# A modulated norm folded into the evacuation of the first projection, at the two places where a whole row must be known first

## The chip, the core and the metric

The kernel runs on one core of a Trainium2 chip. The metric is the device time of one execution in microseconds (us). TensorE (PE in the profile) multiplies matrices into PSUM; VectorE (DVE), ScalarE (ACT) and GpSimd (POOL) do the rest; SyncE (SP) issues the DMAs. Each engine works through its own instructions in their order.

## The reference, cut to what matters

Two blocks of two layers each run on 256 tokens of width 2048, in float32. The first block ends in `rmsnorm(x, norm_f)`. The second block then does, with `c` a conditioning vector:

```
shift, scale, gate = split(silu(c) @ ada_w[i] + ada_b[i], 3)
h = rms_norm(x, norm_g[i]) * (1 + scale) + shift
layer 0:  u, v, z = split(h @ a_w_in, 3);  out = (gelu(u) * mix(layer_norm(gelu(v))) * silu(z)) @ a_w_out
layer 1:  h_kv = rms_norm(x, kv_norm_g) * (1 + kv_scale) + kv_shift
          c_kv, k_r = split(h_kv @ kv_w_dkv);  c_q, z = split(h @ b_w_in);  attention ... @ b_w_out
x = x + gate * out
```

So `h @ W` needs, for each token, the root mean square of a whole row of `x`, and the last quarter of that row comes out of the projection just before it.

## The kernel before

Every float32 product is made of three matmuls: each factor is split into a high part (float32r) and a low part, and `mm3` (L307, L308, L309) adds high by high, low weight by high, and high weight by low. Weights come in chunks of two 128-row tiles by 512 columns (512 KB). A chunk is one step of a `Stream`: twelve matmuls, two tiles by two token halves (t = 0, 1) by three products. A projection onto 512 columns is eight steps, and its result is two PSUM banks (one per half). Each step begins with `begin()`, which writes for the engines, in this order: the high part of a later chunk (L254, ACT, tile wh), due tasks (`after(d, ...)` puts a task d steps ahead), one waiting transpose set (`trq`), the low part of that chunk (L264, DVE, tile wl), due conditioning multiplications (L428, the products silu(c) @ ada_w done on DVE row by row from 512 KB pieces, araw), and DMA fetches. wh and wl are made `ahead` chunks early (4 normally) and have five buffers each; raw weights (wraw) have five as well, which some of the conditioning pieces share. `clk["rate"]` is the number of conditioning pieces fetched per step; when all are read, the generator `ada_gen` is at its end.

Two places need the norm of a whole row while the next projection is due. Both are written as a `crossing` of two streams with half t = 1 lagging two steps. The first goes from `ob3` (the last projection of block 1) to `gv0` and `gv1`, whose chunks alternate in pairs; the second from `go13` to `cq` and `z0`. In it, `evac` adds the residual and squares, `stats` sums the squares and takes the power on POOL, `row_bcast` (L806) spreads the factor over partitions with a matmul (tile inv_row), `evac_tr` transposes the last block (L376, tiles x3tr and x4tr), and `mod_split` multiplies by the factor (L817, tile hx), adds the shift and splits into high (L821, hgH or h2H) and low (L824, hgL or h2L). Between the two crossings `ahead` is 4, inside them it is 2. In the second one the same is done for the key/value input (kv2H, kv2L), then follow `dkv`, the narrow `dkr` (48 matmuls), the query projections `uq` and the key/value projections `ukv`, which need `lora_norm` of cq and of dkv (transposes cqtr, ckvtr).

Of the kernel before, what the change touches and what calls it, by code (L numbers as in the profile page):

```python
# [46 lines left out]
def tile_kernel(ctx: ExitStack, tc: tile.TileContext, A: dict, out: bass.AP):  # L47
# [99 lines left out]
    plan_pair(a_w_in, GW, a_w_in, GW + NB, 8)  # L147
    for j in range(2, 8):
        plan(a_w_in, GW + j * NB)
# [249 lines left out]
    for i in range(2):  # L399
        gd = dram.tile([1, D], F32, name=f"gate{i}")  # L400
        gates.append(gd)

    def store_row(src, dst, name):

        def cp(pt):
            row = T2(nm(name))
            dve.tensor_copy(row[:16, :P], pt[:16, 0, :])
            after(1, lambda: sp.dma_start(dst[0].rearrange("(k p) -> k p", p=P), row[:16, :P]))
        through(3, name, lambda pt: pe.transpose(pt[:16, 0, :], src, ident), cp)
# [3 lines left out]
    def ada_vec(key, W, n0):  # L413
# [5 lines left out]
        def part(j, half):  # L419
# [7 lines left out]
            def mul():  # L427
# [3 lines left out]
                if (j, half) == (15, 1):  # L431
                    if key[:2] == "ga":
                        store_row(d, gates[int(key[2])], "gate_row")
                    done.add(key)
# [5 lines left out]

    def ada_all():
        for key, W, n0 in (("sh0", adaw[0], 0), ("sc0", adaw[0], D), ("ga0", adaw[0], 2 * D),
                           ("kvsh", A["kv_ada_w"], 0), ("kvsc", A["kv_ada_w"], D),
                           ("sh1", adaw[1], 0), ("sc1", adaw[1], D), ("ga1", adaw[1], 2 * D)):
            yield from ada_vec(key, W, n0)

# [357 lines left out]
    def row_bcast(r, pb):  # L804

        pe.matmul(pb, r[:, 0:1].to_broadcast([P, P]), ident, start=True, stop=True)  # L806
        return pb

    def mod_split(z, rbs, sh, H, L, ts, k0, k1):

        w = len(ts) * P
        t0 = ts[0] * P
        n = 4 // len(ts)
        for ka in range(k0, k1, n):
            tmp = T2(nm("hx")).rearrange("p (a b) -> p a b", a=n)
            for i, t in enumerate(ts):
                dve.tensor_mul(tmp[:, :, i * P:(i + 1) * P], z[:, ka:ka + n, t * P:(t + 1) * P],  # L817
                               rbs[t].unsqueeze(1).to_broadcast([P, n, P]))
            for i in range(n):
                k = ka + i  # L820
                act.activation(H[:, k, t0:t0 + w], tmp[:, i, :], AF.Identity, bias=sh[:, k:k + 1])  # L821
            for i in range(n):
                k = ka + i
                dve.scalar_tensor_tensor(L[:, k, t0:t0 + w], tmp[:, i, :], sh[:, k:k + 1],  # L824
                                         H[:, k, t0:t0 + w].bitcast(F32), op0=OP.add, op1=OP.subtract)

    def crossing(s0, s1, z, sh, evac, evac_tr, stats, fin, then=lambda i, rbs: None):

        n0, n1 = len(s0.order), len(s1.order)
        rbs = []
        pb = sc_p.tile([P, 1024], F32, tag="sc", name=nm("inv_row"))
        pieces = {1: ((0,), 4, 8), 2: ((1,), 0, 4), 3: ((1,), 4, 8),
                  5: ((0, 1), 8, 10), 6: ((0, 1), 10, 12), 7: ((0, 1), 12, 14), 8: ((0, 1), 14, 16)}
        clk["ahead"] = LAG
        for i in range(len(s0)):
            if i == n0:  # L840
                evac(s0.ps[0][0], 0)
            if i == n0 + 1:
                rbs.append(stats(0, pb[:, 0:P]))
                evac_tr(0)
            s0.step(i)
        evac(s0.ps[0][1], 1)
        mod_split(z, rbs, sh, s1.H, s1.L, (0,), 0, 4)
        rbs.append(stats(1, pb[:, NB:NB + P]))
        evac_tr(1)
        for i in range(n1 // 2 + 1):  # L850
            if i in pieces:
                mod_split(z, rbs, sh, s1.H, s1.L, *pieces[i])
            s1.step(i)
        last = max(i for i, o in enumerate(s1.order) if o[0] == 0)
        for i in range(n1 // 2 + 1, len(s1)):
            then(i - n1 // 2 - 1, rbs)
            s1.step(i)
            if i == last + s1.lag:
                fin(0, s1.ps[0])
        fin(1, s1.ps[1])  # L860
        clk["ahead"] = AHEAD

    x3d = dram.tile([S, D], F32, name="x3d")
    z3 = B16(F32, "z3")
    ssq2, ssq3 = [ST(f"ssq_x2{t}") for t in range(T)], [ST(f"ssq_x3{t}") for t in range(T)]
# [3 lines left out]
    class Ob:  # L869
# [23 lines left out]
        def evac_tr(self, t):  # L893
            cols_mul(z3, transpose_block(self.xf[t], "x3tr"), gm0[0], self.j, t)

        def whole(self, ps):
            def go():
                for t in range(T):
                    self.evac(ps[t], t)
                for t in range(T):  # L900
                    tr_then(2 + t, self.xf[t], "x3tr", lambda pt, t=t: cols_mul(z3, pt, gm0[0], self.j, t))
            after(1, go)

    def stats_f(t, pb):

        s = ST(nm("s23"))
        dve.tensor_reduce(s[:, 0:1], ssq2[t][:, :4], axis=AX.X, op=OP.add)
        dve.tensor_scalar(s[:, 2:3], s[:, 0:1], EPS / D, EPS * EPS, op0=OP.mult, op1=OP.add)
        dve.tensor_reduce(s[:, 1:2], ssq3[t][:, :4], axis=AX.X, op=OP.add)
        dve.scalar_tensor_tensor(s[:, 2:3], s[:, 1:2], 1.0 / D, s[:, 2:3], op0=OP.mult, op1=OP.add)  # L910
        pool.tensor_tensor(s[:, 3:4], s[:, 2:3], mhalf[:, 0:1], op=OP.pow)
        inv1.append(rstd(s[:, 0:1], 1, D, "inv_f"))
        return row_bcast(s[:, 3:4], pb)
# [14 lines left out]
    clk["rate"] = 0.0  # L928
    ob = Ob(3, 6)
    hH, hL = B16(F32R, "hgH"), B16(F32R, "hgL")  # L930
    vg = [big.tile([P, GW], F32, tag="b16", name=f"vg{t}") for t in range(T)]
    bst = [const.tile([P, 8, 6], F32, name=f"bst{t}") for t in range(T)]

    def gv_evac(j, ps):
        js = slice(j * NB, (j + 1) * NB)

        def gelu():
            for t in range(T):
# [5 lines left out]
        after_each(1, gelu, bn)  # L944
# [18 lines left out]
    for j in range(2, 8):  # L963
# [55 lines left out]
    def lora_norm(ps, gname, name, fast=False):  # L1019
# [6 lines left out]
        def copy():  # L1026
            for t in range(T):
# [34 lines left out]
    class Go:  # L1062
# [23 lines left out]
        def evac_tr(self, t):  # L1086
            pt = transpose_block(self.xb[t], "x4tr")
            cols_mul(z1, pt, gms[1], self.j, t)
            cols_mul(zk, pt, gms[0], self.j, t)

        def whole(self, ps):
            def cols(t, pt):
                cols_mul(zk, pt, gms[0], self.j, t)
                cols_mul(z1, pt, gms[1], self.j, t)

            for t in range(T):
                after(1, lambda t=t: self.evac(ps[t], t))
# [46 lines left out]
    zk, z1 = B16(F32, "zk"), B16(F32, "z1")  # L1144

# [460 lines left out]
```

## Time and profile before

| quantity | value |
|---|---|
| median of 3 runs | 2146.68 us (2146.36 to 2148.63) |
| the profiled execution | 2146.95 us, its span 2145.2 us |
| mean granted TensorE clock | 0.994 of full speed |
| PE, weight loads, DVE, ACT, POOL busy | 98%, 81%, 73%, 47%, 1% of the span |
| instructions | 26773 |
| DMA | 538.27 MB, mean 251 GB/s |

The span runs from the first to the last instruction; the execution has 1.75 us around it. Busy shares are means over stages, and matmuls overlap in the record (each lasts 0.39 us and starts 0.23 us after the one before), so a busy PE says little by itself: what counts is where the start of one matmul is late.

### The profile page before, as it was taken

The numbers are of one execution on the slowest core, as the hardware profiler recorded it, in microseconds if no ns is written. First come the engines' busy times: TensorE is split into PE (matmuls) and PEld (weight loads), VectorE is DVE, ScalarE is ACT, GpSimd is POOL, SyncE is SP. The second block draws the span as 40 slices with busy tenths as digits, with TensorE's granted clock in tenths as the row PEclk, the third lists the DMA queues.
The fourth block names the chain that finished last, engine by engine and source line by source line (L and its number), as shares of the span: only waits on it lengthen the run. The fifth ranks groups of instructions, "written<-read, shape, count | busy, mean of one in ns | idle before, by whom it ended". The sixth has DMA issues, their size and how long they took to land.

```text
span 2145.2 us, 26773 instructions
## 1 busy us (share of the span) xinstructions
PE 2097.5 (98%) x9646; PEld 1729.2 (81%) x9646; DVE 1564.8 (73%) x2277; ACT 1011.6 (47%) x1364; POOL 31.0 (1%) x25
## 2 busy tenths in 40 slices
PE   8999999999999999998999999999999988999999
PEld 6888888888888888886788888888888866788787
DVE  6677788877776776675688888878888767666555
ACT  6444454444545444554544444434344445666442
POOL 0000000000000000000000000000000000110000
PEclk9999999999999999999999999999999999999999
DMA  8788987898755554575699889899889845444455
GB/s 323 277 290 298 307 293 275 300 337 286 245 195 197 187 196 153 188 264 202 219 354 339 316 293 322 316 315 338 286 312 324 279 152 163 150 136 130 128 175 177
DMA packets 157733, 538.27 MB, mean 251 GB/s; under 512 B 17792, under 2 KB 18848, under 8 KB 157088
## 3 DMA queue, kind: packets, MB, share of 16 engines
q1 hardware_dynamic: 157600, 536.56, 72.7%
q8 instruction: 76, 1.25, 0.2%
q14 instruction: 57, 0.47, 0.1%
HBM read 525.99 MB, written 10.50 MB: 250 GB/s over the span
## 4 chain that ended last, share of the span: by engine, by line
PE 52%; DVE 3%; ACT 2%; issue 1%; POOL 0%; ACTq 0%; POOLq 0%; DVEq 0%
PE gz L309 3%; PE gz L307 3%; PE gu L307 3%; PE gu L309 3%; PE gz L308 3%; PE gu L308 3%; PE go L309 3%; PE go L307 3%; PE go L308 3%; PE gv L308 2%; PE gv L309 2%; PE gv L307 2%; PE o L309 1%; PE o L308 1%; PE o L307 1%; PE ob L307 1%
## 5 line engine op out<-in xcount | busy, mean ns | idle before, releaser
L254 ACT ACTIVATE wh<-wraw 128x1024 fp32r<-128x1024 f32 (+2 forms) x698 | 734.4, 1054 | 1031.3 <-issue 145.7
L264 DVE TENSOR_TENSOR wl<-wraw,wh 128x1024 fp32r<-128x1024 f32 (+2 forms) x698 | 846.8, 1218 | 399.6 <-ACT wh L254 395.2
L428 DVE CUSTOM_DVE_ANT_0 araw<-araw,silu_c,vec 128x1024 f32<-128x1024 f32 x128 | 163.8, 1280 | 3.3 <-DMA araw<-in_ada_w 3.1
L307 PE MATMUL q<-wh,hbH 128*128 128x512 f32 x384 | 155.3, 405 | 0.0
L309 PE MATMUL q<-wh,hbL 128*128 128x512 f32 x384 | 150.4, 392 | 0.0
L308 PE MATMUL q<-wl,hbH 128*128 128x512 f32 x384 | 149.7, 390 | 0.0
L308 PE MATMUL gv<-wl,hgH 128*128 128x512 f32 x256 | 100.7, 393 | 1.8 <-DVE wl L264 1.8
L307 PE MATMUL gu<-wh,hgH 128*128 128x512 f32 x256 | 102.0, 398 | 0.0
L307 PE MATMUL gz<-wh,hgH 128*128 128x512 f32 x256 | 101.6, 397 | 0.0
L307 PE MATMUL gv<-wh,hgH 128*128 128x512 f32 x256 | 100.7, 393 | 0.4 <-ACT hgH L821 0.4
L307 PE MATMUL go<-wh,gyH 128*128 128x512 f32 x256 | 100.8, 394 | 0.0
L309 PE MATMUL gv<-wh,hgL 128*128 128x512 f32 x256 | 100.2, 391 | 0.0
L309 PE MATMUL gz<-wh,hgL 128*128 128x512 f32 x256 | 99.9, 390 | 0.0
L309 PE MATMUL go<-wh,gyL 128*128 128x512 f32 x256 | 99.9, 390 | 0.0
L309 PE MATMUL gu<-wh,hgL 128*128 128x512 f32 x256 | 99.7, 390 | 0.0
L308 PE MATMUL go<-wl,gyH 128*128 128x512 f32 x256 | 99.7, 389 | 0.0
L308 PE MATMUL gz<-wl,hgH 128*128 128x512 f32 x256 | 99.7, 389 | 0.0
L308 PE MATMUL gu<-wl,hgH 128*128 128x512 f32 x256 | 99.6, 389 | 0.0
L309 PEld LDWEIGHTS q<-wh,hbL 128*128 128x128 f32 x384 | 72.1, 188 | 15.9
L308 PEld LDWEIGHTS q<-wl,hbH 128*128 128x128 f32 x384 | 72.4, 188 | 13.6
L307 PEld LDWEIGHTS q<-wh,hbH 128*128 128x128 f32 x384 | 72.4, 188 | 13.4
L308 PEld LDWEIGHTS gv<-wl,hgH 128*128 128x128 f32 x256 | 48.5, 189 | 12.9 <-DVE wl L264 3.1
(370 smaller groups left out, 4401.4 us busy)
## 6 DMA issues: line engine op xcount, KB each, us to landing
araw<-in_ada_w SPq DMA_DIRECT2D x192, 512.0 KB, 5.6
wraw<-in_a_w_in SPq DMA_DIRECT2D x192, 512.0 KB, 5.3
wraw<-in_w_in_b SPq DMA_DIRECT2D x128, 512.0 KB, 4.1
araw<-in_kv_ada_w SPq DMA_DIRECT2D x64, 512.0 KB, 5.6
wraw<-in_a_w_out SPq DMA_DIRECT2D x64, 512.0 KB, 5.5
wraw<-in_w_in_a SPq DMA_DIRECT2D x63, 512.0 KB, 6.0
wraw<-in_b_w_in SPq DMA_DIRECT2D x40, 512.0 KB, 3.5
wraw<-in_w_out_a SPq DMA_DIRECT2D x32, 512.0 KB, 5.7
```

The source lines that it names most:

```text
L254: act.activation(h, raws[c], AF.Copy)
L264: dve.tensor_sub(l, raws.pop(c), parts[c][0].bitcast(F32))
L307: pe.matmul(p[:, :nn], hH[:, k, ts], wh[:, j, :nn], start=start, stop=False)
L308: pe.matmul(p[:, :nn], hH[:, k, ts], wl[:, j, :nn], start=False, stop=False)
L309: pe.matmul(p[:, :nn], hL[:, k, ts], wh[:, j, :nn], start=False, stop=stop)
L428: dve.tensor_tensor_reduce(out=w, in0=w, in1=sc[:, half * 1024:(half + 1) * 1024], scale=1.0, scalar=d[:, j:j + 1] if half else bias[:, j: ...
```

## The change

Both crossings go. `ob3` and `go13` become ordinary projections. While they and their predecessors are evacuated, the columns that go into z3 (or z1) without the factor are also split into high and low (`raw_split`, tiles x3H/x3L and x5H/x5L). The next projection, `gv0` or `cq`, takes these unnormed parts. Since `h = r * z + shift` for a row factor r, its result is `r * (z @ W) + shift @ W`: `shifted` multiplies each PSUM half by r and adds the row `shift @ W`, in one DVE instruction per half. That row is made beforehand by `ada_shift`, from a second copy of the 512 columns of weights laid out transposed (sh_w0, sh_w1): eight 512 KB pieces for each of the two, multiplied by the shift vector on DVE after the vectors sc0 and sc1, stored to DRAM and read back broadcast. Class `Mod` makes the spread factor and splits the normed input for the projections after it, a pair of tiles per task, at steps of their own; `gv1` (and `dkv`, then `z0`) take that. `z0` moves behind `dkr`, `consts_2` and `rope_gain` some steps on. `ahead` stays 4. `store_row` gets four more uses, each a narrow transpose, a copy and a store.

```diff
-    plan_pair(a_w_in, GW, a_w_in, GW + NB, 8)
-    for j in range(2, 8):
+    for j in range(8):
         plan(a_w_in, GW + j * NB)
...
-    plan_pair(b_w_in, 0, b_w_in, NB, 8)
+    plan(b_w_in, 0)
     plan(A["w_dkv"], 0)
     PLAN.append((A["w_dkr"], KT, 64))
+    plan(b_w_in, NB)
...
+        def part(q, jp, row):
+            clk["ada"] += 1
+            w = wp.tile([P, CK * NB], F32, tag="wraw", name=nm("sraw"), bufs=5).rearrange("p (j n) -> p j n", j=2)
+            sp.dma_start(w, W[q, jp])
+
+            def mul():
+                for jj in range(2):
+                    a = d[:, 2 * jp + jj:2 * jp + jj + 1]
+                    dve.tensor_tensor_reduce(out=w[:, jj], in0=w[:, jj], in1=row, scale=1.0, scalar=a if q else 0.0,
+                                             op0=OP.mult, op1=OP.add, accum_out=a)
...
+    def raw_split(z, H, L, j, t):
+
+        ks, ts = slice(4 * j, 4 * j + 4), slice(t * P, (t + 1) * P)
+        split_to(H[:, ks, ts], L[:, ks, ts], z[:, ks, ts])
+
+    class Mod:
...
+        def split(self, z, sh, H, L, k):
+            tmp = T2(nm("hx")).rearrange("p (a b) -> p a b", a=2)
+            dve.tensor_mul(tmp, z[:, k:k + 2, :], self.rb.unsqueeze(1).to_broadcast([P, 2, S]))
+            for i in range(2):
+                act.activation(H[:, k + i, :], tmp[:, i, :], AF.Identity, bias=sh[:, k + i:k + i + 1])
+
+            def lows():
+                for i in range(2):
+                    dve.scalar_tensor_tensor(L[:, k + i, :], tmp[:, i, :], sh[:, k + i:k + i + 1],
+                                             H[:, k + i, :].bitcast(F32), op0=OP.add, op1=OP.subtract)
+            after(1, lows)
...
+    def shifted(ps, r, row):
+
+        for t in range(T):
+            dve.scalar_tensor_tensor(ps[t], ps[t], r[t], row, op0=OP.mult, op1=OP.add)
...
-    crossing(Stream(["ob3"], mH, mL, KT, chunks(KT), lag=LAG),
-             Stream(["gv0", "gv1"], hH, hL, KT, pair_order(8), lag=LAG),
-             z3, ada["sh0"], lambda p, t: ob.evac(p, t), ob.evac_tr, stats_f, gv_evac)
+    def norm_f():
+        mod0.append(Mod(stats_f(), lambda m: m.all(0, 1.3, z3, ada["sh0"], hH, hL)))
+    mod0, row0 = [], []
+    after(2, norm_f)
+    after(5, lambda: row_load(0, row0))
+    ps = proj(rH, rL, KT, "gv0")
+    after(1, lambda: shifted(ps, mod0[0].r, row0[0]))
+    gv_evac(0, ps, 2)
...
+    def norm_4():
+        def then(m):
+            m.all(0, 1.2, zk, ada["kvsh"], kvH, kvL)
+            m.all(10, 1.2, z1, ada["sh1"], hH, hL)
+        mod1.append(Mod(stats_4(), then))
+    after(2, norm_4)
+    after(5, lambda: row_load(1, row1))
+    after(10, consts_2)
+    after(14, rope_gain)
+    ps = proj(rH, rL, KT, "cq")
+    qc = lora_norm(ps, "g_qa", "cq", lambda: shifted(ps, mod1[0].r, row1[0]))
     dkv = proj(kvH, kvL, KT, "dkv")
```

PE at the first norm, before: the last matmuls of ob3 (tile ob, high and low input mgH, mgL), the factor's matmul on the identity (ident), the transposes of the last evacuated block, and the first of gv0.

```order
L308 MATMUL ob_1569_7916<-wl_7982,mgH 128x512
L309 MATMUL ob_1569_7916<-wh_7979,mgL 128x512
L806 MATMUL inv_row_7904<-ident,s_1597_8075 128x128
L376 MATMUL x3tr_8086<-ident,xf_8060 128x128 x4
L307 MATMUL ob_1569_7916<-wh_7998,mgH 128x512
L308 MATMUL ob_1569_7916<-wl_8006,mgH 128x512
...
L309 MATMUL ob_1569_7916<-wh_7998,mgL 128x512
L806 MATMUL inv_row_7904<-ident,s_1603_8113 128x128
L376 MATMUL x3tr_8124<-ident,xf_8100 128x128 x4
L307 MATMUL gv_1607_8131<-wh_8022,hgH 128x512
```

The same place now: the transposes and the factor's matmuls (tile rbc) stand among the matmuls of gv0 on the unnormed x3H and x3L, in its third and fourth step.

```order
L309 MATMUL gv_1614_8147<-wh_8069,x3L 128x512
L383 MATMUL x3tr_8213<-ident,xf_8139 128x128 x4
L307 MATMUL gv_1613_8146<-wh_8089,x3H 128x512
L308 MATMUL gv_1613_8146<-wl_8091,x3H 128x512
...
L309 MATMUL gv_1614_8147<-wh_8089,x3L 128x512
L850 MATMUL rbc_8241<-ident,r_1617_8167 128x128
L850 MATMUL rbc_8241<-ident,r_1621_8178 128x128
L307 MATMUL gv_1613_8146<-wh_8107,x3H 128x512
L308 MATMUL gv_1613_8146<-wl_8109,x3H 128x512
```

Before, PE had nothing to do between the factor's two matmuls but the rest of ob3; now 36 matmuls of gv0 stand ahead of them.

DVE while gv0 and gv1 run, before: multiplication by the factor, four low parts, and one weight chunk in turn.

```order
L817 TENSOR_TENSOR hx_8161<-z_7257,inv_row_7904 128x512
L824 SCALAR_TENSOR_TENSOR hgL<-hx_8161,ada_sh_562,hgH 128x128 x4
L264 TENSOR_TENSOR wl_8174<-wraw_8044,wh_8171 128x1024
L817 TENSOR_TENSOR hx_8190<-z_7257,inv_row_7904 128x512
L824 SCALAR_TENSOR_TENSOR hgL<-hx_8190,ada_sh_562,hgH 128x128 x4
L264 TENSOR_TENSOR wl_8202<-wraw_8067,wh_8200 128x1024
```

Now, in steps 12 to 15 counted from the start of gv0 (the last four multiplications by rb are hx_8390 to hx_8496): the conditioning pieces (L430) stand there too, the last low parts behind three of them.

```order
L858 TENSOR_TENSOR hx_8447<-z_7288,rb_8184 128x512
L864 SCALAR_TENSOR_TENSOR hgL<-hx_8419,ada_sh_566,hgH 128x256 x2
L264 TENSOR_TENSOR wl_8454<-wraw_8372,wh_8445 128x1024
L430 ISA araw_8415,ada_kvsh<-araw_8415,silu_c,vec 128x1024
...
L264 TENSOR_TENSOR wl_8477<-wraw_8401,wh_8473 128x1024
L430 ISA araw_8443,ada_kvsh<-araw_8443,silu_c,ada_kvsh 128x1024
...
L858 TENSOR_TENSOR hx_8496<-z_7288,rb_8184 128x512
L264 TENSOR_TENSOR wl_8500<-wraw_8429,wh_8494 128x1024
L430 ISA araw_8471,ada_kvsh<-araw_8471,silu_c,vec 128x1024
...
L864 SCALAR_TENSOR_TENSOR hgL<-hx_8496,ada_sh_566,hgH 128x256 x2
```

The low part of a pair of tiles now stands a step behind its multiplication, with a weight chunk and up to one conditioning piece between them.

PE behind the second norm: what follows the last matmul of dkr, before (first block) and now (second block).

```order
L1223 MATMUL dkr<-kv2L,wh_14424 64x256
L307 MATMUL uq_2842_14593<-wh_14454,more 128x384
L308 MATMUL uq_2842_14593<-wl_14456,more 128x384
L309 MATMUL uq_2842_14593<-wh_14454,more 128x384
L307 MATMUL uq_2843_14594<-wh_14454,more 128x384
```

```order
L1260 MATMUL dkr<-kv2L,wh_14306 64x256
L307 MATMUL z_2844_14522<-wh_14335,h2H 128x512
L308 MATMUL z_2844_14522<-wl_14360,h2H 128x512
L309 MATMUL z_2844_14522<-wh_14335,h2L 128x512
L307 MATMUL z_2845_14523<-wh_14335,h2H 128x512
```

The eight steps of z0 now lie between dkr and the first query projection.

## Rows read from the trace of the kernel before

**Rows 1.** What PE waited for, whole program: us in total, times, longest.

```profile
PE inv_row L806 <- POOL s L911: 9.0, 2, 5.1
PE inv_row L806 <- POOL inv_r L195: 8.3, 2, 4.8
...
PE ukv L307 <- ACT ckvH L369: 2.5, 2, 1.9
```

**Rows 2.** Busy time by stretch: both norms, a steady stretch, an earlier one, one at half clock.

```profile
core 0: us, PE busy (x) PEld busy (x) DVE busy (x) ACT busy (x) POOL busy (x), PEclk, DMA share, GB/s
976.53:1061.03 84.50, 73.37 (x310) 58.79 (x309) 52.73 (x86) 40.70 (x67) 2.11 (x4) 0.94 0.52 173
1061.03:1191.58 130.55, 130.55 (x577) 108.15 (x576) 110.19 (x132) 56.82 (x60) 2.01 (x1) 1.00 0.95 347
1715.88:1837.07 121.19, 104.69 (x462) 83.75 (x460) 79.20 (x139) 58.24 (x99) 2.48 (x4) 0.94 0.50 162
...
402.21:490.23 88.02, 88.02 (x394) 72.88 (x393) 70.47 (x87) 38.43 (x40) 0.00 (x0) 1.00 0.90 330
...
1851.90:1855.10 3.20, 3.20 (x10) 2.05 (x9) 2.12 (x6) 1.06 (x1) 1.22 (x1) 0.50 0.17 37
```

**Rows 3.** The chain that ended last, in gv0 and gv1: start, duration, work.

```profile
1029.36 1.23 DVE wl L264
1030.58 0.67 DVE hx L817 x2
...
1033.17 1.23 DVE wl L264
```

**Rows 4.** PE in order of time around one set of transposes: start, duration.

```profile
962.23 0.40 PE L309 MATMUL ob<-wh,mgL 128*128 128x512 f32 x1
962.46 0.60 PE L383 MATMUL x3tr<-ident,xf 128*128 128x128 f32 x4
...
963.60 0.39 PE L307 MATMUL ob<-wh,mgH 128*128 128x512 f32 x1
```

**Rows 5.** DVE in order of time, where it ran without a wait: start, duration.

```profile
947.00 0.68 DVE L886 TENSOR_TENSOR xb<-ob,xb 128x512 f32<-128x512 f32 x1
...
949.66 1.22 DVE L264 TENSOR_TENSOR wl<-wraw,wh 128x1024 fp32r<-128x1024 f32 x1
...
960.38 0.69 DVE L802 TENSOR_TENSOR z<-x3tr,ada_sc 128x512 f32<-128x512 f32 x1
960.99 1.22 DVE L264 TENSOR_TENSOR wl<-wraw,wh 128x1024 fp32r<-128x1024 f32 x1
962.12 1.28 DVE L428 CUSTOM_DVE_ANT_0 araw<-araw,silu_c,vec 128x1024 f32<-128x1024 f32 x1
...
963.32 0.69 DVE L802 TENSOR_TENSOR z<-x3tr,ada_sc 128x512 f32<-128x512 f32 x1
...
1780.98 0.88 DVE L824 SCALAR_TENSOR_TENSOR kv2L<-hx,ada_kvsh,kv2H 128x256 fp32r<-128x256 f32 x2 [0.58 <-ACT kv2H L821]
1781.78 0.75 DVE L817 TENSOR_TENSOR hx<-zk,inv_row 128x256 f32<-128x256 f32 x2
...
1845.75 0.68 DVE L1040 TENSOR_TENSOR hx<-ckvtr,vec 128x512 f32<-128x512 f32 x1
...
1847.74 1.22 DVE L264 TENSOR_TENSOR wl<-wraw,wh 128x1024 fp32r<-128x1024 f32 x1
```

**Rows 6.** The nearest group to `shifted`: busy us, mean ns, idle before.

```profile
L1080 DVE SCALAR_TENSOR_TENSOR xb<-xb,inv_f_r,yb 128x512 f32<-128x512 f32 x8 | 6.0, 752 | 0.3
```

**Rows 7.** PE in order of time: dkr's first, uq's first, two waits of ukv.

```profile
1831.62 0.28 PE L1221 MATMUL dkr<-kv2H,wh 128*64 128x256 f32 x1
...
1837.07 0.33 PE L307 MATMUL uq<-wh,more 128*128 128x384 f32 x1
...
1847.15 0.50 PE L307 MATMUL ukv<-wh,ckvH 128*128 128x512 f32 x1 [0.62 <-ACT ckvH L369]
...
1850.27 0.50 PE L307 MATMUL ukv<-wh,ckvH 128*128 128x512 f32 x1 [1.90 <-ACT ckvH L369]
```

**Rows 8.** DMA issues: tile, engine, times, KB each, median us to landing.

```profile
wraw<-in_a_w_in SPq DMA_DIRECT2D x192, 512.0 KB, 5.3
```

More of the change, by code (lines that the diff above doesn't have):

```diff
@@ L401, in tile_kernel, with store_row @@
         gates.append(gd)
[L403 removed]
+    shd = [dram.tile([1, D], F32, name=f"shift{i}") for i in range(2)]
+    shWd = [dram.tile([1, NB], F32, name=f"shiftW{i}") for i in range(2)]
+    def store_row(src, dst, name, n=16):
         def cp(pt):
             row = T2(nm(name))
[L407 to L409 removed]
+            dve.tensor_copy(row[:n, :P], pt[:n, 0, :])
+            after(1, lambda: sp.dma_start(dst[0].rearrange("(k p) -> k p", p=P), row[:n, :P]))
+        through(3, name, lambda pt: pe.transpose(pt[:n, 0, :], src, ident), cp)
     done = set()
@@ L439, in ada_vec, with ada_shift @@
                 yield
+    def ada_shift(i, W):
+        d = ST(f"sh_dot{i}")
+        def part(q, jp, row):
[7 more added lines that the diff above has]
+                                             op0=OP.mult, op1=OP.add, accum_out=a)
+                if (q, jp) == (3, 1):
+                    store_row(d[:, :4], shWd[i], "shW_row", 4)
+                    done.add(f"shW{i}")
+            slow.append((clk["s"] + 2, mul))
+        for q in range(4):
+            row = T2(nm("sh_row"))
+            sp.dma_start(row, bcast_rows(shd[i][0, q * NB:(q + 1) * NB], NB))
+            for jp in range(2):
+                part(q, jp, row)
+                yield
     def ada_all():
@@ L827, in crossing @@
[L827 to L861, printed above, removed]
@@ new lines, in raw_split, with __init__, fill, copy @@
+    def raw_split(z, H, L, j, t):
+        ks, ts = slice(4 * j, 4 * j + 4), slice(t * P, (t + 1) * P)
+        split_to(H[:, ks, ts], L[:, ks, ts], z[:, ks, ts])
+    class Mod:
+        def __init__(self, r, then):
+            self.r, self.then = r, then
+            self.rb = T2(nm("rb"))[:, :S]
+            through(1, "rbc", self.fill, self.copy)
+        def fill(self, pt):
+            for t in range(T):
+                pe.matmul(pt[:, t, :], self.r[t].to_broadcast([P, P]), ident, start=True, stop=True)
+        def copy(self, pt):
+            act.activation(self.rb, pt[:, :T, :].rearrange("p a b -> p (a b)"), AF.Copy)
+            self.then(self)
+        def split(self, z, sh, H, L, k):
[8 more added lines that the diff above has]
+            after(1, lows)
+        def all(self, d, every, z, sh, H, L):
+            for i in range(8):
+                if d + int(i * every):
+                    after(d + int(i * every), lambda i=i: self.split(z, sh, H, L, 2 * i))
+                else:
+                    self.split(z, sh, H, L, 2 * i)
@@ L1153, in tile_kernel @@
     go = Go(1, 3, 4)
+    go.whole(proj(gH, gL, KT, "go13"))
     clk["rate"] = 0.0
```

122 lines of the change are left out of this document (59 added, 63 removed).

## The prediction

> **What bounds the kernel now.** I read the granted clock and the busy shares first, then the waits of PE, then the stretches. In a steady stretch PE is the bound: six projections take 130.55 us [rows 2], so 21.76 us each, 2.72 us per step of twelve matmuls and 0.2267 us per matmul. That stretch runs at full clock with the DMA engines 0.95 busy, and no engine waits long enough there to hold PE. The list of waits then says where PE stands still: on the factor's matmul, 9.0 us at the first norm and 8.3 us at the second, and 2.5 us at the key/value projections [rows 1]. The reader should not take these 17.3 us for the price of the norms. The windows show more: ob3, gv0 and gv1 take 84.50 us where three projections at the steady pitch take 65.28, an excess of 19.2 us; go13, cq, z0, dkv and dkr take 121.19 us [rows 2] where four projections and dkr's 5.45 us [rows 7] would take 92.5, an excess of 28.7 us. The rest of the excess has two parts. The mean clock is 0.94 in both stretches, so there PE was at half clock for a while behind each stop. And behind the stop PE is not the bound: one step of gv0/gv1 takes 3.81 us from one weight chunk to the next on DVE [rows 3] against 2.72, because multiplication, ACT's high part, DVE's low part and the next chunk wait for each other. DVE is only 52.73 us busy in the 84.50 us: a chain, not a full engine. So what the change has to remove is this chain, and the question is what comes next there.
>
> **First norm.** Both halves of ob3's last block, the factor's matmuls and the split no longer stand ahead of gv0: its first twelve input tiles are split already, and the four of the last block, transposed in its third and fourth step, are due in its seventh. PE's work is three projections, 65.28 us, plus four sets of transposes. One set adds 0.46 us: 1.37 us between two matmuls that have four matmuls (0.91) and the set between them [rows 4]. So 1.84 us, and about 0.4 for the two factor matmuls (an estimate: nothing to one set, a little under the set). The wait of the factor's matmul for DVE's sums and POOL's power stays in PE's order, with gv0's steps 4 to 8 queued behind it. Its cover is gv0's first three steps, 8 us; DVE reaches the sums about 6.5 us after gv0's start by the ledger below. Were that cover gone, the longest old wait, 5.1 us [rows 1], is its price.
>
> What is late next, I think, is DVE. gv1 needs all of the normed input by its last chunk, and DVE makes it between. I add up DVE's start-to-start times from gv0's second step to the last low part (pair 7, issued in step 15): 14 weight chunks at 1.14 = 16.0; one evacuation 2.66; eight multiplications at 0.61 = 4.9; eight pairs of low parts at 0.80 = 6.4; two blocks of z with its raw split at 2.0 = 4.0; six conditioning pieces at 1.20 = 7.2 [rows 5]; `shifted`, two instructions as the 752 ns one, about 1.45 [rows 6]. Ten sums and scalings on a few columns and two `bn_stats` have no row: I take 1.3 and 1.2, the last as two multiplications, the first near nothing; the bounds for both are 0 and 0.61 each. Sum 45.1 us. PE reaches that chunk after 15 steps, 40.8 us, plus two transpose sets and the factor, 1.3, plus 0.45 for the matmuls of the chunk that still need only the high part: 42.6. So DVE is late by 2.5 us. Earlier low parts (pairs 4 to 6) meet their steps within a microsecond. A PE stop of 1.90 us [rows 7] was followed by 3.20 us at half clock [rows 2], a loss of 1.6, so I add a little more, 1.7, for this one. Sum: 65.28 + 1.84 + 0.4 + 2.5 + 1.7 = 71.7 against 84.50: **12.8 us gained**.
>
> `shifted` waits on DVE for gv0's last matmul; behind it are that step's weight chunk and low parts. Weights are made four chunks, 10.9 us, ahead, so a chunk may be that late; the low parts are the term above. ACT waits for each multiplication with the next weight's high part queued behind it, under the same lead.
>
> **Second norm.** go13, cq, dkv and z0: 4 x 21.76 = 87.04, dkr 5.45 [rows 7], eight transpose sets (four of x4, two each of cq and the key/value latent) 3.68, the factor 0.4, the rope transposes 0.5, and 0.7 for z0's second PSUM bank, which is dkv's and comes free only when ACT has copied dkv (estimate between nothing and one ACT-wait of 1.90 [rows 7]). Sum 97.8 against 121.19: **23.4 us gained**. The input of dkv is due 5 to 13 steps after cq's start and that of z0 ten steps later, so the same ledger, spread over 24 steps and dkr, ends about 69 to 71 us after its start where PE's need is about 71.7. Not late, with a margin of 1 to 3 us. The constants that move here are five DMAs and twelve small DVE instructions; they are in it.
>
> **Behind it.** The latents are now normed while z0 runs, so the waits of the key/value projections on ACT go, 2.5 us [rows 1], their 1.6 us of half clock, and 1.4 us of transposes that are counted above: **5.5 us gained**.
>
> **Costs.** Four `store_row` transposes, narrow, between nothing and a set each: at most 1.8, I take **1.6**. The two rows `shift @ W` take 16 pieces of 512 KB and eight small row DMAs. They go in as conditioning pieces do, at the same number per step, so that gates and later vectors come later but no step has more. On DVE a piece is two half-size instructions, about 1.4 us for 1.20 [rows 5]; DVE has room: 110.19 of 130.55 us in the busiest stretch. SP issues them ahead of the next weight fetch, whose chunk has five buffers and takes 5.3 us to land [rows 8]. What hides them is PE's lead of four chunks, and stretches with the DMA engines 0.90 and 0.95 busy [rows 2] ran without a stop. Price nothing; without that cover see the last rival.
>
> Sum: 2145.2 - 12.8 - 23.4 - 5.5 + 1.6 = 2105.1 us of span; 1.75 us lie around it: 2106.9. The profiled execution, 2146.95 us, is 0.27 above the median of the runs, so I say **2107**.
>
> **A rule against the rows.** Whether DVE is late by 2.5 us hangs on how close two instructions stand. Rows: a multiplication of 0.69 us is followed after 0.61, a chunk of 1.22 after 1.13, so the next starts before the last has ended [rows 5]. The Trainium skill, page "VectorE: DVE Perf Modes", section "The DRAIN you can't avoid", says that the next operation does not start until the pipe is empty; its section on two instructions with no wait between them lets one that is not held start earlier, which is what these rows show. By the first rule the sum would be the first rival's below, by the rows it is the one above.
>
> **Rivals.**
> 1. DVE's instructions stand back to back at their full durations. Then the 40-odd of the ledger take some 0.1 us more each and end at 49.7: 7.2 us late in place of 2.5, and at the second norm about 1 late with 1.7 us of half clock: 2107 + 4.7 + 2.7 = 2114.5. For it: most of these have a semaphore between them and ACT. Against: rows 5 show the overlap with different tiles on either side. The section named above is this rule.
> 2. DVE is not late at all, because pieces slip (each waits for its DMA and yields its place) or the stop is under a step: 2107 - 2.5 - 1.7 = 2102.8, say 2102. For it: DVE's margin is 2 us in 45. Against: the order puts three conditioning pieces ahead of the last low parts.
> 3. The change does not do at the second norm what it does at the first: DVE, ACT and the buffers go round at 3.81 us a step as now [rows 3], for the sixteen steps that split: 16 x 1.09 = 17.5 more: 2124.5. Against: a split is now two steps long, not one, and with `ahead` 4.
> 4. Slower than before: the pieces of the second weight copy take the weight buffers, five in all, and PE waits for a landing of 5.3 us [rows 8] each time: 16 x 5.3 = 85, so 2192. It decides at 40 / 16 = 2.5 us a piece. For it: they and the chunks share the buffers, and the DMA engines are 0.9 busy there. Against: a buffer is held about 8 us (landing and one step), so five pass 1.7 tiles a step where 1.75 are wanted for some eleven steps, a deficit of half a tile against a lead of four chunks.
>
> **Chances and range.** The forecast 0.55, rival 1 0.15, rival 2 0.20, rival 3 0.07, rival 4 0.03. The range must leave out no more than 0.2: from 2099 (rival 2 with the 1.6 of the transposes and 2 us of bank and factor estimates at nothing) to 2120 (rival 1 with the bank's 1.90 and the sums at their upper bound of 0.61 each, 4 us). Rivals 3 and 4 and the tails stay outside, about 0.15 together. 0.2% is 4.3 us, about what a measurement of this kernel can tell from no change; all cases but rival 4 lie well below it, so faster 0.95, same 0.02, slower 0.03.
>
> **What the profile should show.** No wait of several microseconds of PE on POOL's power. gv0 and cq at 22 to 23 us. One stop of PE in gv1's last chunk on DVE's low part (hgL), about 2.5 us, and a stretch at half clock behind it; rival 2 has none, rival 1 a long one. z0 and dkv free of such stops; if they show stops at each step, rival 3 is right. No wait of ukv on ckvH. No wait on weights while the shift pieces are read (from about 400 to 490 us, and again near 1510 to 1560); any there is rival 4's. The forecast is wrong if DVE's spacing there is not that of rows 5, or if some wait that the order puts on PE, above all the factor's, is not covered by the steps ahead of it.

## The result, and the profile after

| | before | after |
|---|---|---|
| median | 2146.52 us (2144.49 to 2148.63, 4 runs) | 2111.44 us (2110.24 to 2115.11, 4 runs) |
| span of the profiled execution | 2145.2 us | 2109.7 us |
| ratio to before | | 0.9839, 95% interval 0.9822 to 0.9856 |
| mean granted clock | 0.994 | 0.998 |

The kernel is faster by 35 us, 1.6%. The forecast was 2107, with a range of 2099 to 2120.

What PE waited for in the whole program after the change (us in total, times, longest), cut to the waits around the two norms:

```profile
PE gv L307 <- ACT hgH L860: 2.5, 1, 2.5
...
PE x3tr L383 <- DVE xf L908: 1.7, 1, 1.7
...
PE gv L309 <- DVE hgL L864: 1.5, 1, 1.5
...
PE x4tr L383 <- DVE xb L1120: 0.8, 2, 0.6
...
PE ckvtr L383 <- ACT ckv L1073: 0.3, 1, 0.3
```

The 17.3 us on the factor and the 2.5 us on ckvH [rows 1] are gone, and the factor's new matmul (rbc) does not appear at all: its cover held. At the first norm POOL had the second factor ready at 1009.16, 1.1 us ahead of the matmul (POOL and PE: start, duration):

```profile
1008.62 0.54 POOL L934 TENSOR_TENSOR r<-s,mhalf 128x1 f32<-128x1 f32 x1
...
1010.22 0.60 PE L850 MATMUL rbc<-ident,r 128*128 128x128 f32 x4
```

In place of the old waits stand 2.5 and 1.5 us in gv1, on the last pair of normed tiles, and 1.7 us in ob2 that no term of the forecast had. Busy times by stretch after the change: ob2; ob3; gv0; gv1; the last three together; go13 to z0; the first uq and ukv.

```profile
core 0: us, PE busy (x) PEld busy (x) DVE busy (x) ACT busy (x) POOL busy (x), PEclk, DMA share, GB/s
953.70:978.39 24.69, 23.03 (x108) 18.82 (x106) 20.69 (x27) 13.21 (x20) 0.00 (x0) 1.00 0.83 287
978.39:1001.12 22.73, 22.73 (x106) 18.81 (x105) 16.94 (x21) 12.33 (x18) 0.00 (x0) 1.00 0.91 317
1001.12:1024.30 23.18, 23.18 (x109) 19.26 (x108) 21.57 (x40) 15.11 (x25) 3.04 (x4) 1.00 0.82 266
1024.30:1051.95 27.65, 23.69 (x97) 18.90 (x96) 27.65 (x40) 14.51 (x21) 2.48 (x1) 0.94 0.78 294
978.39:1051.95 73.56, 69.60 (x309) 56.97 (x308) 66.17 (x98) 41.94 (x64) 5.52 (x5) 0.98 0.83 292
1707.38:1806.43 99.05, 98.11 (x473) 80.96 (x471) 83.78 (x136) 61.91 (x105) 4.91 (x5) 1.00 0.63 205
1806.43:1852.03 45.60, 44.44 (x220) 37.87 (x218) 32.28 (x62) 31.70 (x63) 7.08 (x3) 1.00 0.60 192
```

ob3, gv0 and gv1 take 73.56 us instead of 84.50 [rows 2], go13 to z0 99.05 instead of 121.19. The row to look at is gv1: DVE is busy 27.65 of 27.65 us, while PE stands 3.96 us and runs at a mean clock of 0.94. DVE, busy 52.73 of 84.50 us around this norm before [rows 2], is now the engine that is full. What it does at the end of gv1 (DVE in order of time: start, duration):

```profile
1038.63 1.27 DVE L430 CUSTOM_DVE_ANT_0 araw<-araw,silu_c,vec 128x1024 f32<-128x1024 f32 x1
...
1041.76 3.03 DVE L430 CUSTOM_DVE_ANT_0 araw<-araw,silu_c,ada_kvsh 128x1024 f32<-128x1024 f32 x1
...
1044.72 0.68 DVE L858 TENSOR_TENSOR hx<-z,rb 128x512 f32<-128x512 f32 x1
1045.32 1.21 DVE L264 TENSOR_TENSOR wl<-wraw,wh 128x1024 fp32r<-128x1024 f32 x1
1046.46 1.27 DVE L430 CUSTOM_DVE_ANT_0 araw<-araw,silu_c,vec 128x1024 f32<-128x1024 f32 x1
...
1047.66 0.87 DVE L864 SCALAR_TENSOR_TENSOR hgL<-hx,ada_sh,hgH 128x256 fp32r<-128x256 f32 x2
```

The last multiplication (1044.72) and the last low part (1047.66) each come behind a conditioning piece. One of these pieces took 3.03 us where its kind takes 1.28. GpSimd has a single instruction there, which cuts the triangle out of the mixing weights wsT:

```profile
1041.23 2.48 POOL L996 TENSOR_SCALAR_AFFINE_SELECT wsT<-wsT 128x2048 f32<-128x2048 f32 x1 [31.57 <-DMA wsT<-in_wsT]
```

PE meets the two late tiles, and the matmuls behind them last up to 0.63 us instead of 0.39 until the clock is back (PE in order of time):

```profile
1045.99 0.50 PE L307 MATMUL gv<-wh,hgH 128*128 128x512 f32 x1 [2.49 <-ACT hgH L860]
...
1048.19 0.80 PE L309 MATMUL gv<-wh,hgL 128*128 128x512 f32 x1 [1.47 <-DVE hgL L864]
...
1049.21 0.63 PE L308 MATMUL gv<-wl,hgH 128*128 128x512 f32 x1
```

gv1's excess over 21.76 us is therefore 5.89: 3.96 of standing and 1.93 of slower matmuls.

### The profile page after: what moved, and what is told of

Read it like the earlier page. It is cut to its first block, busy times and chain, and to the rows that moved or that the text cites. A ratio compares the mean times of both kernels' runs of the same rounds, so it can differ in the third digit from the quotient of the medians.

```text
span 2109.7 us, 26909 instructions
## 1 busy us (share of the span) xinstructions
PE 2084.6 (99%) x9650; PEld 1723.2 (82%) x9650; DVE 1588.3 (75%) x2333; ACT 1018.8 (48%) x1366; POOL 34.2 (2%) x25
## 3 DMA queue, kind: packets, MB, share of 16 engines
q8 instruction: 76, 1.25, 0.2%
## 4 chain that ended last, share of the span: by engine, by line
PE 51%; DVE 3%; DMA 1%; ACT 1%; issue 1%; POOL 0%; SPq 0%; DVEq 0%; ACTq 0%
PE gz L309 3%; PE gz L307 3%; PE gu L309 3%; PE gz L308 3%; PE gu L307 3%; PE gu L308 3%; PE gv L309 2%; PE gv L307 2%; PE gv L308 2%; PE go L307 2%; PE go L309 2%; PE go L308 2%; PE o L307 1%; PE o L308 1%; PE o L309 1%; PE z L307 1%
## 5 line engine op out<-in xcount | busy, mean ns | idle before, releaser
L430 DVE CUSTOM_DVE_ANT_0 araw<-araw,silu_c,vec 128x1024 f32<-128x1024 f32 x128 | 163.8, 1280 | 6.8 <-DMA araw<-in_ada_w 6.6
L307 PE MATMUL gv<-wh,hgH 128*128 128x512 f32 x224 | 87.7, 392 | 2.5 <-ACT hgH L860 2.5
L309 PE MATMUL gv<-wh,hgL 128*128 128x512 f32 x224 | 87.9, 392 | 1.5 <-DVE hgL L864 1.5
L308 PE MATMUL gv<-wl,hgH 128*128 128x512 f32 x224 | 87.6, 391 | 0.0
L307 PE MATMUL u<-wh,haH 128*128 128x512 f32 x128 | 51.8, 405 | 5.7 <-ACT wh L254 5.7
```

Of the source, the lines that this page charges most:

```text
L307: pe.matmul(p[:, :nn], hH[:, k, ts], wh[:, j, :nn], start=start, stop=False)
L308: pe.matmul(p[:, :nn], hH[:, k, ts], wl[:, j, :nn], start=False, stop=False)
L309: pe.matmul(p[:, :nn], hL[:, k, ts], wh[:, j, :nn], start=False, stop=stop)
L430: dve.tensor_tensor_reduce(out=w, in0=w, in1=sc[:, half * 1024:(half + 1) * 1024], scale=1.0, scalar=d[:, j:j + 1] if half else bias[:, j: ...
```

## The experiments

All are edits of the changed kernel, and none leaves out a part of the output. A time stands beside 2111.4 of the changed kernel, and ratios are to the kernel before on the same chip.

**GpSimd's instruction, first try (e1).** The theory: the piece of 3.03 us and GpSimd's instruction held each other up. The rival: the piece was long for a reason of its own.

```diff
-    after(8, tri_ws)
+    after(20, tri_ws)
```

> The triangle that GpSimd cuts into wsT (L996) is issued twelve steps later, in gv2 and gv3 instead of in gv1; nothing else changes. Theory A: that instruction ran from 1041.23 to 1043.71 us, and the DVE conditioning piece that started at 1041.76 took 3.03 us instead of 1.28 because the two engines got in each other's way; DVE was already full in gv1, so the last high and low parts came 1.75 us later than by its own work. Then no piece in gv1 is longer than 1.4 us, PE's stops in gv1 fall from 3.96 us to about 2.2, gv1 from 27.65 to 25.0 (with less half clock), and the time from 2111.4 to about 2109. Theory B: the piece was long for a reason of its own (its data, its place), GpSimd has nothing to do with it: a piece of 3 us stays in gv1, gv1 stays at 27.6 and the time at 2111.4.

Measured 2111.42 us (2110.51 to 2114.7). The edit did not do what it was for: GpSimd has nothing else in its queue there, so its instruction still started when the data of wsT had landed, and a piece beside it again took 3.03 us; gv1 took 27.63.

```profile
1038.66 3.04 POOL L996 TENSOR_SCALAR_AFFINE_SELECT wsT<-wsT 128x2048 f32<-128x2048 f32 x1 [31.02 <-DMA wsT<-in_wsT]
...
1039.75 3.03 DVE L430 CUSTOM_DVE_ANT_0 araw<-araw,silu_c,ada_kvsh 128x1024 f32<-128x1024 f32 x1
```

It decides nothing between the two theories. It shows that here the wait for the data set the time of the instruction, and not the step of its issue.

**GpSimd's instruction, with its load (e5).**

```diff
-    after(4, load_ws)
-    after(8, tri_ws)
+    after(16, load_ws)
+    after(20, tri_ws)
```

> Now the load of wsT is issued twelve steps later too, on which GpSimd's instruction waits, so it runs in gv2 or gv3. Theory A (the two engines hold each other up): no DVE instruction in gv1 is lengthened, one in gv2 or gv3 takes some 1.8 us more than its kind; PE's stops in gv1 fall from 3.96 us to about 2.2, gv1 from 27.65 to 25 or 25.5, the time from 2111.4 to about 2109. Theory B (the piece in that place is long whatever GpSimd does): a piece of 3 us stays in gv1, gv1 stays at 27.6.

Measured 2107.91 us (2106.81 to 2108.4), ratio 0.9815 (0.9802 to 0.9829). Waits of PE, gv1's window, and GpSimd and DVE in gv3:

```profile
PE gv L309 <- DVE hgL L864: 1.5, 1, 1.5
...
PE gv L307 <- ACT hgH L860: 0.7, 1, 0.7
```

```profile
1024.39:1048.91 24.52, 22.34 (x97) 17.86 (x96) 24.52 (x37) 14.50 (x21) 0.00 (x0) 1.00 0.77 270
```

```profile
1074.66 2.01 POOL L996 TENSOR_SCALAR_AFFINE_SELECT wsT<-wsT 128x2048 f32<-128x2048 f32 x1 [64.93 <-DMA wsT<-in_wsT]
```

```profile
1074.31 1.28 DVE L969 BATCH_NORM_STATS2 bst<-vg 128x6 f32<-128x512 f32 x2
1075.51 2.23 DVE L264 TENSOR_TENSOR wl<-wraw,wh 128x1024 fp32r<-128x1024 f32 x1
```

The long DVE instruction went where GpSimd's instruction went; there it took 1.0 us more than its kind, where 1.8 was expected. In gv1 the same piece, now at 1041.82, took 1.28 us with the same instructions around it. The stops in gv1 fell by 1.8 us, as expected, to 2.2. gv1 fell by 3.13 us to 24.52, more than expected, since the clock stayed at 1.00. The rival falls.

**No conditioning pieces in gv0 and gv1 (e2).** Theory: DVE's queue is late. Rival: the last pair passes to and fro between ACT and DVE too slowly, whatever else DVE does.

```diff
     mod0, row0 = [], []
+    clk["rate"] = 0.0
     after(2, norm_f)
...
-    clk["rate"] = 0.78
+    clk["rate"] = 0.0
...
     for j in range(1, 8):
         gv_evac(j, proj(hH, hL, KT, f"gv{j}"))
+        clk["rate"] = 0.96
```

> No conditioning piece is fetched while gv0 and gv1 run; the eight or nine that are left out there are fetched in gv2 to gv7 (rate 0.96 in place of 0.78). Theory A (DVE's queue is what is late in gv1): some 7 us of pieces leave DVE ahead of the last low part, which was 4 us late; PE has no stop in gv1, the clock stays full, gv1 takes 21.8 to 22 us, the time is 2105 to 2106. Theory B (the last pair is late because ACT and DVE pass each tile to and fro, whatever else DVE does): stops of 2 us or more stay in gv1 and the time is 2109 or above. Theory C (the denser pieces in gv2 to gv7 take the DMA engines): gv1 is free, but gv2 to gv7 rise above 21.76 us each and the gain is lost there.

Measured 2105.5 us (2104.3 to 2108.41), ratio 0.9808 (0.9792 to 0.9824), as the theory said. Windows of gv1 and of gv2 to gv7:

```profile
1022.65:1044.41 21.76, 21.76 (x98) 18.03 (x96) 20.17 (x27) 13.88 (x19) 2.99 (x1) 1.00 0.69 223
...
1044.41:1174.97 130.56, 130.56 (x578) 108.15 (x576) 116.69 (x147) 56.84 (x60) 0.00 (x0) 1.00 0.98 372
```

gv1 runs at PE's pitch although GpSimd's instruction still lies in it, and one pair of low parts took 2.62 us instead of 0.87:

```profile
1033.21 2.62 DVE L864 SCALAR_TENSOR_TENSOR hgL<-hx,ada_sh,hgH 128x256 fp32r<-128x256 f32 x2
```

With some 7 us less in its queue (six pieces of 1.20) DVE can bear that. And the denser pieces cost gv2 to gv7 nothing, at a DMA share of 0.98.

**ob's first transposes two steps later (e3).**

```diff
-                    tr_then(1 + t, self.xf[t], "x3tr", lambda pt, t=t: out(t, pt))
+                    tr_then((1 if self.j else 3) + t, self.xf[t], "x3tr", lambda pt, t=t: out(t, pt))
```

> The transposes of ob's first block (and with them its multiplication by the modulation and its split) are issued two steps later, behind the evacuation of the second block. Theory A: the 1.7 us for which PE's x3tr waited for DVE's xf at 956 us came from the new split of the first block, which stood on DVE ahead of that evacuation; the wait goes, ob2 falls from 24.69 us to about 23.2, the time by 1.5 us to about 2110. Theory B: DVE has too much to do there in any order, the wait only moves to another transpose of ob2 or ob3, and the time stays at 2111.4 within 0.5.

Measured 2110.37 us (2108.91 to 2112.91): by itself not to be told from 2111.4. The profile says more. The 1.7 us wait is gone (0.2 left), and ob1 and ob2 take 47.00 us together instead of 48.35. But gv1 takes 28.29 instead of 27.65. That is not the wait moved on: PE's stops in gv1 fell from 3.96 to 3.5 us, and the last low part let it go on 23.88 us after gv1's start, against 23.89 in the changed kernel. The matmuls behind were slower, at a mean clock of 0.88 in gv1 instead of 0.94. So theory A holds for the place of the wait, and half of the gain went in the clock.

**Both (e6), and with a later narrow transpose (e10).** e6 joins the edits of e2 and e3. e10 adds to them a parameter of `store_row`, so that the transpose of the row `shift @ W` stands ten steps behind the last piece instead of three.

```diff
-    def store_row(src, dst, name, n=16):
+    def store_row(src, dst, name, n=16, d=3):
...
-        through(3, name, lambda pt: pe.transpose(pt[:n, 0, :], src, ident), cp)
+        through(d, name, lambda pt: pe.transpose(pt[:n, 0, :], src, ident), cp)
...
-                    store_row(d[:, :4], shWd[i], "shW_row", 4)
+                    store_row(d[:, :4], shWd[i], "shW_row", 4, 10)
```

> No conditioning pieces fetched in gv0 and gv1, and the first block's transposes of ob two steps later: both edits that took a wait from PE. Theory A (two separate places on DVE): the gains add, about 5.9 and 1.5, since the half microsecond by which gv1 grew when the transposes alone were moved finds room now: 2104. Theory B (the later transposes only push DVE's work into gv0 and gv1): gv1 shows a stop again and the time is that without the pieces, 2105.5, or above.

> Single pieces; no conditioning pieces in gv0 and gv1, ob's first transposes two steps later, and the narrow transpose ten steps behind the last piece. In the version without the last edit PE stood 1.5 us on that transpose at the second norm's row. Theory A: that stop and its half clock go, 2103.7 falls to 2101 to 2102.5. Theory B: the last piece's landing is seen elsewhere (on a weight chunk), 2103.7 within 0.5.

e6: 2103.74 us (2101.75 to 2106.78), ratio 0.9795 (0.9781 to 0.9808); gv1 took 21.76. This is below the changed kernel beyond both intervals, and about the sum of the two gains. It showed a new wait of PE:

```profile
PE shW_row L411 <- DVE sh_dot L457: 1.5, 1, 1.5
```

e10 removed that wait and its profiled span was 2100.4 us against e6's 2105.1, but its runs gave 2105.4 us (2102.14 to 2109.51), ratio 0.9805 (0.9792 to 0.9818): from e6 it can't be told apart, and its theory is not shown by the times.

**What covers the pieces of the second weight copy (e7, e9).** In the changed kernel the two v projections in which the first eight pieces lie take 21.76 and 21.91 us, so there the pieces and the row's narrow transpose cost some 0.15 us. Are they free, or nearly not? e7 doubles them in place.

```diff
                 part(q, jp, row)
+                w2 = wp.tile([P, CK * NB], F32, tag="wraw", name=nm("sraw2"), bufs=5).rearrange("p (j n) -> p j n", j=2)
+                sp.dma_start(w2, W[q, jp])
+                def again(w2=w2, row=row):
+                    for jj in range(2):
+                        dve.tensor_tensor_reduce(out=w2[:, jj], in0=w2[:, jj], in1=row, scale=1.0, scalar=0.0,
+                                                 op0=OP.mult, op1=OP.add, accum_out=d[:, 8 + jj:9 + jj])
+                slow.append((clk["s"] + 2, again))
                 yield
```

> Each of the 16 pieces of the second weight copy is fetched and multiplied twice, the second time into columns that nothing reads, in the same step and with the same five weight buffers: what the pieces cost is doubled at the same places. Theory A (hidden under the lead of four chunks): the projections in which they lie (two of v, some of gu and gz) stay at their lengths within 0.2 us, the time at 2111.4 to 2112. Theory B (they take buffers from the weights, at a deficit that is only just covered): PE waits for wh there, 2 to 5 us for each of the two places, 2115 to 2121.

Measured 2135.56 us (2130.41 to 2140.18): 24 us slower, beyond the 2121 of theory B too, so theory A fell. PE's waits there:

```profile
PE shW_row L411 <- DVE sh_dot L457: 12.3, 2, 7.3
...
PE v L308 <- DVE wl L264: 2.4, 2, 2.2
```

Most of PE's standing was a thing that neither theory had: the narrow transpose stands in PE's order and waits, through DVE's last sum, for the last piece to land. In the changed kernel itself this is close. DVE's last sum and PE's transpose there:

```profile
462.89 0.75 DVE L457 CUSTOM_DVE_ANT_0 sraw<-sraw,sh_row,sh_dot 128x512 f32<-128x512 f32 x1
```

```profile
464.34 0.27 PE L411 MATMUL shW_row<-ident,sh_dot 128*4 128x128 f32 x1
```

The sum ends at 463.64, 0.7 us ahead of the transpose. So e9 gives the doubled version the later transpose too, by the same diff as e10.

> The doubled pieces again, but the narrow transpose that turns shift @ W into a row is issued ten steps behind the last piece in place of three. With the doubled pieces PE stood 5.0 and 7.3 us on that transpose, which waits for DVE's last sum and so for the last piece's landing, and 2.4 us on weights. Theory A (the pieces hold PE only through that transpose): the two stops and their half clock go, the time falls from 2135.6 to 2112 to 2116, what is left being the 2.4 us on weights. Theory B (the pieces take buffers and transfers from the weights, and the transpose merely came first in PE's order): the stops move to wh and wl, and the time stays above 2125.

Measured 2134.99 us (2133.45 to 2135.64). Now the stops are on the weights, and ACT's own waits in that stretch say on what (PE in the whole program, then all engines from 420 to 500 us):

```profile
PE v L308 <- DVE wl L264: 6.7, 3, 3.8
...
PE gz L308 <- DVE wl L264: 3.7, 5, 1.9
PE gytr L383 <- DVE gz L1165: 2.9, 1, 2.9
```

```profile
ACT wh L254 <- DMA wraw<-in_w_v: 27.5, 11, 5.2
```

Theory B holds: pieces take buffers and transfers from the weights, and the transpose had only come first in PE's order. With 16 pieces this price is nearly nothing in these two places, with 32 it is some 24 us in the whole. Where between the two it begins was not measured.

**z0 back ahead of dkv (e4).** The weights' plan and the two calls of `all` change places with it (z1 first, zk ten steps later).

```diff
+    z_evac(0, proj(hH, hL, KT, "z0"))
     dkv = proj(kvH, kvL, KT, "dkv")
...
-    z_evac(0, proj(hH, hL, KT, "z0"))
```

> z0 goes back ahead of dkv, as in the kernel before, with its weights and with its input split first and the key/value input ten steps later. Theory A: z0 behind dkr is what covers the norms of the key/value latent; without it PE waits again for ckvH and its transposes, 2.5 us and more with half clock behind it, less 0.7 us for the PSUM bank that z0 waited for: slower by 3.5 to 6 us, 2115 to 2117.5, the loss lying between the first uq and the end of the second ukv. Theory B: the 5 us that were gained behind the second norm come from the different order of the splits and transposes, not from where z0 stands: within 1 us of 2111.4.

Measured 2116.88 us (2114.66 to 2119.34), 5.4 slower by the medians and 3.8 by the profiled spans (2113.5 and 2109.7); the ranges of the two kernels overlap a little. The waits of before are back, and so is the length of the first uq and ukv, 50.34 us instead of 45.60:

```profile
PE ukv L307 <- ACT ckvH L369: 2.5, 2, 1.9
...
PE dkv L309 <- DVE kv2L L864: 1.5, 2, 1.2
```

```profile
1805.57:1855.91 50.34, 47.84 (x230) 39.72 (x229) 35.27 (x67) 33.83 (x72) 7.77 (x4) 0.97 0.46 147
```

z0's place is what covers the key/value latent's norm: that stretch is 4.7 us longer, with the clock at 0.97 again. The stretch from cq to the first uq takes 75.40 us against 75.38 in the changed kernel, but not because the other order is free: PE waits 1.5 us there for dkv's input, and ten transposes, 1.1 us, have left it for the next stretch.

**The first norm alone (e8).** The second norm is the crossing of before, without its second weight copy.

```diff
-    plan(b_w_in, 0)
+    plan_pair(b_w_in, 0, b_w_in, NB, 8)
     plan(A["w_dkv"], 0)
     PLAN.append((A["w_dkr"], KT, 64))
-    plan(b_w_in, NB)
...
-            if key[:2] == "sc":
+            if key == "sc0":
...
+    crossing(Stream(["go13"], gH, gL, KT, chunks(KT), lag=LAG),
+             Stream(["cq", "z0"], hH, hL, KT, pair_order(8), lag=LAG),
+             z1, ada["sh1"], lambda p, t: go.evac(p, t), go.evac_tr, stats_4, firsts, kv_mod)
...
-    ps = proj(rH, rL, KT, "cq")
-    qc = lora_norm(ps, "g_qa", "cq", lambda: shifted(ps, mod1[0].r, row1[0]))
...
```

> Only the first norm is changed; the second is the crossing of before, with its weights in pairs and without its second weight copy. Theory A (the two places are independent): the first norm gives 10.9 us in ob3, gv0 and gv1, less 1.7 lost in ob2 and 0.3 for the rows: about 9, so 2138; the second part then shows its 121 us again. Theory B (they depend on each other, since the first moves the conditioning pieces and what comes due at the second): a gain that differs from 9 by more than 2 us, with the second crossing at another length than 121 us.

Measured 2138.97 us (2137.06 to 2141.3) against 2147.34: 8.4 us faster. ob3, gv0 and gv1 take 73.79 us, the second crossing 121.49, as before. As far as these times tell, the two places are independent, and the second gives three quarters of the gain.

## Why the prediction was right, and where it was off

Its time was 4.6 us low by the profiled spans. By its terms:

| term | forecast | measured |
|---|---|---|
| ob3, gv0, gv1 | 71.7 | 73.56 |
| of that, PE standing in gv1 | 2.5 | 3.96 |
| of that, half clock behind it | 1.7 | 1.93 |
| go13 to z0 | 97.8 | 99.05 |
| gained in the first uq and ukv | 5.5 | 5.1 |
| costs elsewhere | 1.6 | 2.6 |

The two rows of before that the last lines rest on, beside [rows 2]: the first uq and ukv, and ob2.

```profile
1837.07:1887.75 50.68, 48.16 (x230) 39.55 (x229) 35.27 (x67) 33.83 (x72) 7.71 (x4) 0.97 0.47 146
...
953.08:976.53 23.45, 23.45 (x111) 19.22 (x110) 18.80 (x24) 11.02 (x16) 0.00 (x0) 1.00 0.91 324
```

**What bound the two places** was read rightly: the excess of 19.2 and 28.7 us is more than the waits of 17.3, and what was gained, 10.9 and 22.1, is more than the waits too. Once the split is not in PE's way, gv0 runs at 23.18 and cq at 23.38 us. One rival stands untested: the new kernel also makes weights four chunks ahead where the crossings did so two ahead, and no run separates this from the fold.

**DVE as what is late next** was right, and is shown by e2 (without the pieces no stop, 5.9 us less). The ledger itself was good: 45.1 us forecast; measured 46.45, from 1002.08 (the start of the evacuation of ob3) to 1048.53, and 1.75 of these are the lengthened piece. The rest is 44.7. Instructions stood as close as in [rows 5]: a multiplication of 0.69 us at 1015.62 is followed at 1016.23. So rival 1 (back to back at full durations) is wrong. The Trainium skill, page "VectorE: DVE Perf Modes", section "The DRAIN you can't avoid", says that the next operation does not start until the pipe is empty, and also that one that is not held starts earlier. This trace agrees with the second: 0.61 us from start to start behind a record of 0.69.

**The term that was mis-sized: "So DVE is late by 2.5 us."** The sum took DVE's instructions at their times without asking what GpSimd does beside them. The load and the triangle of wsT are counted in steps from the point in the program that follows the norm; that was gv2's start and is now gv1's. So they came into the critical stretch, and a piece stood still for 1.75 us. e5 measures it: 3.13 us in gv1, of which 1.78 are stops and the rest slower matmuls. Rival 2's case (nothing late) was wrong too: with the collision gone 2.2 us of stops remain, close to the 2.5 of the ledger. The 1.7 us at half clock beside it came out near (1.93) by luck: without the collision, in e5, the clock stayed at 1.00 and PE's busy time was only 0.6 us above the pitch (22.34 against 21.76). That this could happen was to be read in the trace of before, where GpSimd's instruction started at 1073.16 and this stood on DVE:

```profile
1073.20 3.05 DVE L264 TENSOR_TENSOR wl<-wraw,wh 128x1024 fp32r<-128x1024 f32 x1 [1.49 <-ACT wh L254]
```

There DVE had room, and PE ran through (130.55 of 130.55 us [rows 2]), so no wait pointed to it.

**A term that was missing:** the raw split of ob's first block stands ahead of the second block's evacuation on DVE, and PE's transpose in ob2 waited 1.66 us for it (DVE's split, then its evacuation, then PE):

```profile
956.19 0.69 DVE L370 TENSOR_TENSOR x3L<-z,x3H 128x512 fp32r<-128x512 f32 x1 [0.70 <-ACT x3H L369]
956.80 0.68 DVE L905 TENSOR_TENSOR xb<-ob,xb 128x512 f32<-128x512 f32 x1
...
958.35 0.63 PE L383 MATMUL x3tr<-ident,xf 128*128 128x128 f32 x4 [1.66 <-DVE xf L908]
```

I had costed the splits as if only gv0 and cq had them. e3 shows the place; ob2 is 1.24 us longer than before, which is half of the 2.6 in the table (1.71 from ob0 to ob2, 0.55 from gu0 to go12, 0.37 ahead of ob0 and behind the first uq and ukv). The narrow transposes, for which I took 1.6, cost little: from gu0 to go12, with two of them and eight of the pieces, the changed kernel needs 524.84 us and the one before 524.29.

**The second norm** was right in mechanism, and in size to 1.25 us. PE stands 0.94 us in it, 0.61 of that in go13, where x4tr waits for DVE's residual. No split stands ahead of that residual, but a conditioning piece that waited 0.87 us for its own transfer (DVE, then PE):

```profile
1708.10 1.28 DVE L430 CUSTOM_DVE_ANT_0 araw<-araw,silu_c,vec 128x1024 f32<-128x1024 f32 x1 [0.87 <-DMA araw<-in_ada_w]
...
1710.03 0.69 DVE L1120 TENSOR_TENSOR xb<-xb,yb 128x512 f32<-128x512 f32 x1
...
1710.87 0.63 PE L383 MATMUL x4tr<-ident,xb 128*128 128x128 f32 x4 [0.61 <-DVE xb L1120]
```

In the kernel before, the last conditioning piece ran at 1688.71, 27 us ahead of go13; now the sixteen pieces of the second weight copy are fetched ahead of the last vector's. By this order the stop is a price of theirs that the forecast put at nothing; no run shows it by itself. No wait on dkv's PSUM bank appears, so no run shows the 0.7 us taken for it; the rest of the difference was not taken apart. Rival 3 is wrong: no stop at each step.

**The pieces** were hidden where they are read, as said, but for a weaker reason than I gave. I named five buffers and a lead of four chunks; half a tile of deficit, I wrote, is nothing against that. Doubling shows that the reserve is less than eight pieces at each place, and that a wait lay 0.7 us away in the order of PE. Rival 4 had its chance too low for a mechanism as near as that.

One bound of the range was added up wrong, without effect: ten sums at 0.61 us are 6.1, so 4.8 above the 1.3 taken and not 4, and by the same terms the upper end is 2114.5 + 1.2 + 4.8 = 2120.5.

## What to carry to other kernels

When a change removes a wait, add up the queue of the engine that makes the now critical data, in order, with everything that stands in it: here the conditioning pieces, which had nothing to do with the norm, cost 5.9 us together with the collision, and fetching them two projections later took this back. Then look at what the other engines run in the same window: here a collision that had cost PE nothing came into a critical place unseen. And price added transfers by doubling them: that the profile showed no wait said nothing here of how near one was.

## What the runs showed of the hardware

GpSimd's select on the 128x2048 tile in SBUF and DVE held each other up. Where it met no DVE instruction with two SBUF inputs under way it took 2.01 us (in the kernel before, and in e5). Where it started during one, it took 2.07 us (e9) to 3.04 us (e1): some 1.95 us of it lie behind the start of the lengthened DVE instruction, 1041.76 to 1043.71 in the changed kernel and 1039.75 to 1041.70 in e1. They did not always take turns: in e2, e6 and e10 a multiplication stood between, took its usual 0.68 or 0.69 us, and the 1.95 us lie behind the start of the instruction after it. And the weight chunk or piece issued while it worked ended 1.07 or 1.08 us behind the select's end: 1043.71 and 1044.79 in the changed kernel, 1075.17 and 1076.25 before, 1076.67 and 1077.74 in e5. The two `bn_stats` that lay beside its start in e5, with one input each, took 1.28 us together, no more than elsewhere (1.29). The Trainium skill, page "SBUF — State Buffer", section "Who interferes with whom", says that a Vector instruction with two SBUF inputs contends with a GpSimd instruction that reads SBUF, that one with at most one SBUF input, outside the 2-port modes, does not, that the lock is exclusive, and that issue order decides who blocks. The traces agree, at 1.0 to 1.8 us a meeting, but for the multiplication that went ahead of the waiting select in e2, e6 and e10.

Nor had I expected the clock's part: 2.2 us of stops in gv1, as 0.7 and 1.5, left it at 1.00 (e5), while 3.96, as 2.49 and 1.47, brought the stretch to 0.94, and 3.5, as 2.5 and 1.0, to 0.88 (e3). Only in the last two did matmuls behind the stops run long at the lower of the clock's two levels, 0.63 us each instead of 0.39.
